# One store of 2 KB tiles for weights and work; output projections over 512 columns with their weights kept for both halves

## The chip, the cores and the metric

The kernel runs on one core of a Trainium2 chip. The metric is the device time of one execution in microseconds (us); the number given for a kernel is the median of its runs. Five engines share the work: TensorE (PE, matrix products, with its weight loads shown apart as PEld), VectorE (DVE), ScalarE (ACT), GpSimd (POOL) and SyncE (SP), which here issues nearly all transfers (DMA). Each engine runs its own instructions in a fixed order and waits on semaphores for the others.

## The reference

Four layers follow one another on one sequence of 1024 tokens of width 1024, all in float32: gated linear attention (gla), spatial gating (sgu), forgetting attention (fox), and gla again.

```python
cond = jax.nn.silu(c)
for i in range(DEPTH):                       # DEPTH = 4
    mod = (cond @ w_mod[i] + b_mod[i])[:, None, :]
    shift, scale, gate = jnp.split(mod, 3, axis=-1)
    h = rms_norm(x, norm_pre_g[i]) * (1.0 + scale) + shift
    kind, j = i % N_MIXERS, i // N_MIXERS
    if kind == 0:
        o = gla_mixer(h, gla_w_in[j], gla_w_a2[j], gla_b_a[j], gla_g_head[j], gla_w_out[j])
    elif kind == 1:
        o = sgu_mixer(h, sgu_w_in[j], sgu_ln_g[j], sgu_ln_b[j], sgu_w_s[j], sgu_b_s[j], sgu_w_out[j])
    else:
        o = fox_mixer(h, fox_w_in[j], fox_b_f[j], fox_g_q[j], fox_g_k[j], fox_w_out[j])
    x = x + gate * rms_norm(o, norm_post_g[i])
```

Each mixer begins with one wide product `h @ w_in` (3,088 columns for gla, 3,072 for sgu, 4,112 for fox) and ends with `(o * silu(z)) @ w_out` (1024 by 1024). These projections are most of the arithmetic. In sgu the `v` part of the product goes through a gelu and a layer norm over all of its 1024 columns.

## The kernel before

**Products.** A float32 product is made of three TensorE products: each operand is split into a high part in a shorter format and the low remainder, and `mm3` (L281) issues high by high (L283), high by low (L284 or L285) and low by high. For the activations the two parts are `hTh` and `hTl`, held for the whole layer, transposed, as 8 slices of 128 features. A token block is 128 tokens (8 of them, four to a half). `proj_tok` gives one token block times some columns of a weight, `proj_feat` gives 128 features times 512 tokens. Either runs over 8 slices `kt`, 24 matmuls in all, into one of three PSUM buffers called `pj`.

**Weights.** A weight is used in blocks of columns, usually 256. `load_w` (L244) brings a block in two pieces of 4 slices each (`wraw`, 128 partitions by 4 by 256, 512 KB, two buffers), ACT copies a piece to its high part `whi` (L252, CAST) and POOL subtracts for the low part `wlo` (L253). The parts lie in a pool of their own, `wp`, with 8 buffers under the tag `whl`. `getw` (L274) hands out the next block that the layer planned and starts the loads and splits of the one after it. The plan of a layer is made when that layer's code begins, so in program order nothing of the next layer's weights is asked for before the last projection of this one.

**Work tiles.** All other short-lived tiles come from a pool `sp` of 28 slots of 2 KB (per partition).

**Output projection.** `out_proj` (L397) goes through the two halves of the tokens; for each it fetches four blocks of 256 columns, so every block is loaded and split twice. For each block and each of 4 token blocks it makes a product of 256 columns, which DVE multiplies by the gate (L408) and ACT squares and sums (L410). When a half is done, `post` (L420) is queued as a filler, to be taken in steps between the products that follow: for each token block it loads `x` (L426), sums (L432), takes a reciprocal root on POOL (`rsq`, L337 and L338), adds to `x` in two pieces of 512 (L436), stores the new `x` (L440), and then starts the next layer's entry: a square and sum on ACT (L350), another `rsq`, a scaling on DVE, transposes on PE (L362) and the writing of `hTh` and `hTl`. So the second half's `post` runs beside the first projection of the next layer. The first projections of a layer need weights and the token blocks of the first half, which are ready by then.

**Order.** The program is built with a scheduler that simulates the engines and decides in which order each engine takes the instructions of the whole program, and when a pool's slot is handed to the next tile. The order on an engine can therefore differ from the order of the code, also across the end of a layer. A transfer waits on SP for the transfer issued eight before it, since there are eight semaphores for them.

## Time and profile before

| quantity | value |
|---|---|
| median of 3 runs | 2219.71 us (2216.93 to 2221.21) |
| profiled execution, device time | 2215.66 us |
| profiled execution, span of its trace | 2213.9 us |
| TensorE busy in the span | 2151.4 us, 97% |
| VectorE busy | 1367.9 us, 62% |
| ScalarE busy | 930.8 us, 42% |
| GpSimd busy | 903.1 us, 41% |
| mean granted TensorE clock | .993 of full speed |
| bytes moved by DMA | 217.54 MB, 98 GB/s |

The profile is of one execution. Busy times of the engines overlap, so they don't add up to the span; the chain of waits, followed back from the last instruction, tells which of them the end of the span rests on. A group in the view by line names line, engine, operation, what is written and read with its shape, the count, then total busy time and mean ns of one, then the idle time of the engine before these instructions and what ended it.

### The profile page before, as it was taken

What the parts mean: (1) busy time and instruction counts of PE and PEld (TensorE: products, weight loads), DVE (VectorE), ACT (ScalarE), POOL (GpSimd) and SP (SyncE); (2) the same over time, 40 slices, a digit from 0 to 9 for tenths busy, and PEclk for the clock granted to TensorE, in tenths of its full rate; (3) what the DMA queues carried; (4) which work ended last, traced back from release to release, by engine and by line L of the source; (5) the groups of instructions that cost most, each with busy time, mean ns of one, the idle gap of its engine ahead of it and who ended that gap; (6) DMA issues with size and microseconds to landing.
All of it is one profiled execution on the core that took longest, in us unless ns stands there. A gap on an engine that the chain in (4) does not pass through costs nothing.

```text
span 2213.9 us, 39277 instructions
## 1 busy us (share of the span) xinstructions
PE 2151.4 (97%) x15173; PEld 1938.8 (88%) x15173; DVE 1367.9 (62%) x3147; ACT 930.8 (42%) x1977; POOL 903.1 (41%) x767
## 2 busy tenths in 40 slices
PE   6999999999999999999999999999999999999998
PEld 6888889999998889998878888888689999899998
DVE  7586879635475425656555656656766675776633
ACT  4644333346321124554444434434556554333342
POOL 5433334366354324655144233232425451342363
PEclk9999999999999999999999999999999999999999
DMA  8122223335425324512222122112325320112334
GB/s 286 46 75 78 86 73 108 121 128 182 130 77 171 122 93 134 179 54 87 79 66 63 60 72 76 58 58 77 99 92 176 127 58 20 48 44 67 115 101 143
DMA packets 178150, 217.54 MB, mean 98 GB/s; under 512 B 13266, under 2 KB 128530, under 8 KB 177962
## 3 DMA queue, kind: packets, MB, share of 16 engines
q1 hardware_dynamic: 177962, 215.02, 30.9%
q8 instruction: 120, 1.97, 0.4%
q14 instruction: 68, 0.56, 0.1%
HBM read 185.03 MB, written 29.95 MB: 97 GB/s over the span
## 4 chain that ended last, share of the span: by engine, by line
PE 84%; DVE 12%; ACT 2%; issue 1%; DMA 1%; POOL 0%; DVEq 0%; POOLq 0%; SPq 0%; ACTq 0%
PE pj L283 21%; PE pj L284 21%; PE pj L285 21%; PE pm L1053 4%; PE pm L1042 3%; PE pb L1017 3%; PE pb L1016 2%; PE pb L621 2%; DVE md L195 2%; DVE s L578 1%; DVE s L610 1%; DVE s L600 1%; DVE s L606 1%; DVE s L603 1%; PE pm L362 1%
## 5 line engine op out<-in xcount | busy, mean ns | idle before, releaser
L283 PE MATMUL pj<-whi,hTh 128*128 128x256 f32 (+1 forms) x3072 | 893.0, 291 | 2.4 <-ACT junk L410 1.9
L285 PE MATMUL pj<-whi,hTl 128*128 128x256 f32 (+1 forms) x3072 | 883.0, 288 | 5.2 <-DVE hTl L385 3.0
L284 PE MATMUL pj<-wlo,hTh 128*128 128x256 f32 (+1 forms) x3072 | 880.9, 287 | 0.0
L253 POOL TENSOR_TENSOR wlo<-wraw,whi 128x1024 fp32r<-128x1024 f32 (+2 forms) x176 | 425.1, 2424 | 436.4 <-ACT whi L252 421.2
L283 PEld LDWEIGHTS pj<-whi,hTh 128*128 128x128 f32 x3072 | 589.0, 192 | 12.4 <-issue 5.1
L285 PEld LDWEIGHTS pj<-whi,hTl 128*128 128x128 f32 x3072 | 588.4, 192 | 12.9 <-issue 4.3
L284 PEld LDWEIGHTS pj<-wlo,hTh 128*128 128x128 f32 x3072 | 589.6, 192 | 6.7 <-issue 3.6
L283 PE MATMUL pj<-hTh,whi 128*128 128x512 f32 x640 | 255.5, 399 | 0.0
L284 PE MATMUL pj<-hTl,whi 128*128 128x512 f32 x640 | 254.4, 398 | 0.0
L285 PE MATMUL pj<-hTh,wlo 128*128 128x512 f32 x640 | 252.6, 395 | 0.0
L252 ACT CAST whi<-wraw 128x1024 fp32r<-128x1024 f32 (+2 forms) x176 | 177.8, 1011 | 133.8 <-PE pj L284 117.8
L195 DVE SCALAR_TENSOR_TENSOR md<-md,cond,md 128x512 f32<-128x512 f32 x184 | 175.3, 954 | 36.2 <-DMA md<-in_w_mod 34.5
L1010 POOL TENSOR_TENSOR db<-s,mneg 128x128 f32<-128x128 f32 x128 | 62.4, 499 | 243.1 <-DVE mx L1025 123.5
L1031 ACT ACTIVATE p<-p,ng 128x256 f32<-128x256 f32 (+7 forms) x128 | 99.6, 778 | 108.1 <-DVE ng L1029 107.2
L284 PEld LDWEIGHTS pj<-hTl,whi 128*128 128x128 f32 x640 | 120.8, 189 | 24.9 <-issue 2.3
L285 PEld LDWEIGHTS pj<-hTh,wlo 128*128 128x128 f32 x640 | 120.7, 189 | 24.8 <-issue 1.1
L283 PEld LDWEIGHTS pj<-hTh,whi 128*128 128x128 f32 x640 | 121.0, 189 | 24.3 <-issue 0.8
L1044 ACT COPY s<-pm 128x512 f32<-128x512 f32 (+2 forms) x192 | 87.1, 481 | 130.2 <-PE pm L1042 125.3
L408 DVE TENSOR_TENSOR s<-pj,gg 128x256 f32<-128x256 f32 x128 | 53.6, 421 | 136.2 <-PE pj L285 136.1
L1020 DVE CUSTOM_DVE_ANT_0 p<-pb,s 128x512 f32<-128x512 f32 (+3 forms) x160 | 83.5, 529 | 73.3 <-PE pb L1017 71.7
L338 POOL TENSOR_TENSOR r<-r,neghalf 128x1 f32<-128x1 f32 (+2 forms) x104 | 111.5, 1078 | 6.6
L410 ACT ACTIVATE junk<-pj 128x256 bf16<-128x256 f32 x128 | 49.2, 384 | 142.5 <-DVE s L408 139.4
(203 smaller groups left out, 3304.6 us busy)
## 6 DMA issues: line engine op xcount, KB each, us to landing
md<-in_w_mod SPq DMA_DIRECT2D x160, 256.0 KB
wraw<-in_gla_w_in SPq DMA_DIRECT2D x32, 512.0 KB
wraw<-in_gla_w_out SPq DMA_DIRECT2D x32, 512.0 KB
yd<-s SPq DMA_DIRECT2D x50, 256.0 KB
xd<-x SPq DMA_DIRECT2D x24, 512.0 KB
wraw<-in_sgu_w_in SPq DMA_DIRECT2D x24, 512.0 KB
x<-xd SPq DMA_DIRECT2D x24, 512.0 KB
wraw<-in_fox_w_in SPq DMA_DIRECT2D x48, 256.0 KB
```

Of the source, the lines that this page charges most:

```text
L195: ins = nc.vector.scalar_tensor_tensor(st["acc"], w[i], self.cond[:, kt:kt + 1], st["acc"], op0=ALU.mult, op1=ALU.add)
L252: nc.scalar.copy(hi, raw)
L253: nc.gpsimd.tensor_tensor(lo, raw, hi.bitcast(F32), op=ALU.subtract)
L283: nc.tensor.matmul(ps, lh, rh, start=first, stop=False)
L284: nc.tensor.matmul(ps, lh, rl, start=False, stop=False)
L285: nc.tensor.matmul(ps, ll, rh, start=False, stop=last)
L338: nc.gpsimd.tensor_tensor(r, r, self.half[:, 0:1].to_broadcast([P, n]) if n > 8 else self.half[:, 0:n], op=ALU.pow)
L1017: nc.tensor.matmul(sp[:, 0:w], q3[2][own[hb], qc], k2[own[hb], 0:w], start=False, stop=True)
L1020: nc.vector.tensor_tensor_reduce(e[:, c * 512:c * 512 + d0], sp[:, 0:d0], nf[p, c, hb][:, 0:d0], op0=ALU.add, op1=ALU.max, scale=1.0, scal ...
L1031: nc.scalar.activation(e[:, 0:n + P], e[:, 0:n + P], AF.Exp, bias=ng, accum_out=ls[:, 0:1])
L1044: nc.scalar.copy(et[:, 0:nb * P], pt[:, 0:nb * P])
L1053: nc.tensor.matmul(po[own[hb], 0:P], v[p, jb // 4][:, jb % 4, hb * 64:hb * 64 + 64], pts[hb][jb // 4][:, (jb % 4) * P:(jb % 4 + 1) * P], s ...
```

## The change

The pools `wp` are gone. One pool `sp` of 49 slots of 2 KB serves work tiles and weights. A block of a weight is loaded in tiles of 512 columns' worth: 4 tiles of two slices by 256 columns, or 8 tiles of one slice by 512, or by 272 where 16 more columns come along (then each tile takes two transfers). Each tile is cast on ACT (L262 after) and subtracted on POOL (L263 after) by itself.

The loads of the next block are no longer all emitted by `getw`; `prefetch` makes a list, and `wemit` takes some of it at slice 3 of each projection, in as many parts as `getw` was told calls. `getw` emits what is left.

`out_proj` works over 2 blocks of 512 columns per half in place of 4 of 256. In gla and sgu the first half's split weights stay in the store for the second half (`stay`), in fox they are loaded again. The `v` part of sgu is made in 512 columns instead of 256, first block for all 8 token blocks and then the second. The 512 KB loads of `w_mod` at the start become two of 256 KB.

Counts over the program: 3840 matmuls of 256 columns become 1920 of 512 (3072 of the 3840 in output projections, 768 in sgu's `v`). POOL's subtractions go from 154 of 1024 columns, 16 of 512 and 6 of 1088 to 276 of 512 and 24 of 272, and ACT's casts alike. The 128 evictions on L408 and the 128 on L410 become 64 each, of 512 columns. The transfers that SP issues rise from 667 to 857.

```diff
-        self.wp = pool("wp", 8)
-        self.sp = pool("sp", 28)
+        self.sp = pool("sp", 49)
...
-    def load_w(self, srcs, now=True):
+    def load_w(self, srcs):
         nc = self.nc
         ncol = sum(s.shape[1] for s in srcs)
-        raws, parts = [], []
...
+        g = max(1, 512 // ncol)
+        parts = {}
+
+        def load(i):
+            raw = self.s2([g, ncol])
             c = 0
             for s in srcs:
                 w = s.shape[1]
                 nc.sync.dma_start(out=raw[:, :, c:c + w],
-                                  in_=s[p4 * 512:(p4 + 1) * 512, :].rearrange("(k p) n -> p k n", p=P))
+                                  in_=s[i * g * P:(i + 1) * g * P, :].rearrange("(k p) n -> p k n", p=P))
                 c += w
...
+        def split(i, raw):
+            hi, lo = self.s2([g, ncol], F32R), self.s2([g, ncol], F32R)
+            nc.scalar.copy(hi, raw)
+            nc.gpsimd.tensor_tensor(lo, raw, hi.bitcast(F32), op=ALU.subtract)
+            parts[i] = (hi, lo)
...
-    def getw(self, ahead=1):
-        while len(self.wdone) < min(self.wnext + 1 + ahead, len(self.wseq)):
-            self.load_w(self.wseq[len(self.wdone)])
+    def prefetch(self, calls):
+        if len(self.wdone) == self.wnext and self.wnext < len(self.wseq):
+            load, split, n = self.load_w(self.wseq[self.wnext])
+            self.wq = [lambda i=i: split(i, load(i)) for i in range(n)]
+            self.wrate = -(-n // calls)
+
+    def wemit(self, n=None):
+        for _ in range(min(n or self.wrate, len(self.wq))):
+            self.wq.pop(0)()
+
+    def getw(self, calls=8, ahead=True):
+        if len(self.wdone) == self.wnext:
+            self.prefetch(1)
+        self.wemit(len(self.wq))
         w = self.wdone[self.wnext]
         self.wnext += 1
+        if ahead:
+            self.prefetch(calls)
         return w
...
     def out_proj(self, li, l, x_src):
...
-            for cb in range(4):
-                w = self.getw()
+            for cb in range(2):
+                if hf and self.stay:
+                    w = ws[cb]
+                    if cb:
+                        self.prefetch(4)
+                else:
+                    w = ws[cb] = self.getw(4, not (self.stay and cb))
                 for t in range(4):
-                    ps = self.proj_tok(w, hf * 4 + t, 256)
+                    ps = self.proj_tok(w, hf * 4 + t, 512, self.tick)
...
         def do_v(g, w, t):                          # sgu
-            ps = self.proj_tok(w, t, 256)
+            ps = self.proj_tok(w, t, 512, self.tick)
...
         for kind, i in order:                       # fox
-            w = self.getw()
+            w = self.getw(2 if kind == "z" else 8)
```

How the scheduler places the work changes at the end of each layer. The place shown is the hand-over from sgu to fox. First SP before: `wraw_9456` and `wraw_9463` are fox's first weights, `x_9527` and the like the token blocks of sgu's last half on their way in (L426) and out (L440).

```order
L426 DMA x_9527<-xd_130 128x1024
L261 DMA wraw_9220<-in_sgu_w_out 128x4x256
L426 DMA x_9529<-xd_130 128x1024
L261 DMA wraw_9456<-in_fox_w_in 128x4x256
L261 DMA wraw_9456<-in_fox_w_in 128x4x16
L261 DMA wraw_9463<-in_fox_w_in 128x4x256
L261 DMA wraw_9463<-in_fox_w_in 128x4x16
L261 DMA wraw_9470<-in_fox_w_in 128x4x128 x2
L261 DMA wraw_9477<-in_fox_w_in 128x4x128 x2
L440 DMA xd_131<-x_9527 128x1024
```

And SP after, where `s_1489_8531`, `s_1492_8538` and so on are fox's first weight tiles, and `x_8654`, `x_8671` and `x_8722` the second, third and fourth token block of sgu's last half (L449 in, L463 out):

```order
L463 DMA xd_128<-x_8654 128x1024
L449 DMA x_8722<-xd_127 128x1024
L463 DMA xd_128<-x_8671 128x1024
L255 DMA s_1489_8531<-in_fox_w_in 128x256
L255 DMA s_1489_8531<-in_fox_w_in 128x16
L255 DMA s_1492_8538<-in_fox_w_in 128x256
L255 DMA s_1492_8538<-in_fox_w_in 128x16
L255 DMA s_1495_8545<-in_fox_w_in 128x256
L255 DMA s_1495_8545<-in_fox_w_in 128x16
L463 DMA xd_128<-x_8722 128x1024
L255 DMA s_1498_8552<-in_fox_w_in 128x256
L255 DMA s_1498_8552<-in_fox_w_in 128x16
```

Fox's first weights stood ahead of every store of sgu's last token blocks; now the first three tiles stand behind the store of the third block and the rest behind that of the fourth. POOL before, at the same place (`wlo_9460` and `wlo_9467` are the low parts of fox's first weights, `r` the roots of `rsq` for sgu's last token blocks):

```order
L253 TENSOR_TENSOR wlo_9223<-wraw_9220,whi_9222 128x1024
L385 TENSOR_TENSOR hTl<-s_1346_9200,hTh 128x4x128
L253 TENSOR_TENSOR wlo_9460<-wraw_9456,whi_9459 128x1088
L253 TENSOR_TENSOR wlo_9467<-wraw_9463,whi_9466 128x1088
L337 TENSOR_SCALAR r_1390_9533<-ss_1389_9531 128x1
L338 TENSOR_TENSOR r_1390_9533<-r_1390_9533,neghalf 128x1
```

And POOL after (`r_1560` belongs to the entry of the third token block, `r_1572` and `r_1575` to the fourth's root and entry):

```order
L353 TENSOR_SCALAR r_1560_8815<-ss_1558_8812 128x1
L353 TENSOR_SCALAR r_1572_8915<-ss_1571_8913 128x1
L354 TENSOR_TENSOR r_1560_8815<-r_1560_8815,neghalf 128x1
L263 TENSOR_TENSOR s_1491_8535<-s_1489_8531,s_1490_8534 128x272
L354 TENSOR_TENSOR r_1572_8915<-r_1572_8915,neghalf 128x1
L263 TENSOR_TENSOR s_1494_8542<-s_1492_8538,s_1493_8541 128x272
L353 TENSOR_SCALAR r_1575_8924<-ss_1573_8921 128x1
L354 TENSOR_TENSOR r_1575_8924<-r_1575_8924,neghalf 128x1
L263 TENSOR_TENSOR s_1497_8549<-s_1495_8545,s_1496_8548 128x272
```

Both subtractions stood ahead of the roots of the last half; now three roots of the last two blocks stand between the first three. Last, PE before, from the last product of sgu (`pj_9415`) to the first of fox (`pj_9499`):

```order
L285 MATMUL pj_9415<-whi_9222,hTl 128x256
L283 MATMUL pj_9499<-whi_9459,hTh 128x272
L284 MATMUL pj_9499<-wlo_9460,hTh 128x272
L285 MATMUL pj_9499<-whi_9459,hTl 128x272
L283 MATMUL pj_9499<-whi_9459,hTh 128x272
```

And PE after (`pj_8490` is sgu's last product, `pm` the transposes of the first block of its last half, `pj_8618`, `pj_8673` and `pj_8724` fox's first three):

```order
L297 MATMUL pj_8490<-s_1420_7995,hTl 128x512
L378 MATMUL pm_8752<-ident,xn_8665 128x128 x4
L378 MATMUL pm_8757<-ident,xn_8665 128x128 x4
L295 MATMUL pj_8618<-s_1490_8534,hTh 128x272
L295 MATMUL pj_8673<-s_1490_8534,hTh 128x272
L295 MATMUL pj_8724<-s_1490_8534,hTh 128x272
L296 MATMUL pj_8618<-s_1491_8535,hTh 128x272
L297 MATMUL pj_8618<-s_1490_8534,hTl 128x272
L296 MATMUL pj_8673<-s_1491_8535,hTh 128x272
```

The first product of fox was made alone, slice after slice; now three token blocks are made side by side, nine matmuls for each weight tile. The hand-overs from gla to sgu and from fox to gla are arranged alike.

## Rows read from the trace of the kernel before

**Rows 1.** The page: busy time of each engine; shares of the chain of waits.
```profile
PE 2151.4 (97%) x15173; PEld 1938.8 (88%) x15173; DVE 1367.9 (62%) x3147; ACT 930.8 (42%) x1977; POOL 903.1 (41%) x767
...
PE 84%; DVE 12%; ACT 2%; issue 1%; DMA 1%; POOL 0%; DVEq 0%; POOLq 0%; SPq 0%; ACTq 0%
```

**Rows 2.** Windows: us, busy PE, PEld, DVE, ACT, POOL, granted clock, DMA, GB/s.
```profile
2150.00:2200.00 50.00, 50.00 (x419) 50.00 (x418) 15.25 (x30) 14.54 (x43) 22.02 (x18) 1.00 0.46 148
```

**Rows 3.** Timeline of PE (start, duration): ends of a 256-wide and a 512-wide run.
```profile
2131.56 0.36 PE L283 MATMUL pj<-whi,hTh 128*128 128x256 f32 x1
...
2206.39 0.28 PE L285 MATMUL pj<-whi,hTl 128*128 128x256 f32 x1
...
637.45 0.39 PE L283 MATMUL pj<-hTh,whi 128*128 128x512 f32 x1
...
658.99 0.39 PE L285 MATMUL pj<-hTh,wlo 128*128 128x512 f32 x1
```

**Rows 4.** Timelines of SP, ACT, POOL and PE at the hand-over from sgu to fox.
```profile
910.64 13.75 SPq L261 DMA_DIRECT2D wraw<-in_fox_w_in  x8
...
926.26 0.34 SPq L440 DMA_DIRECT2D xd<-x  x1
...
917.21 1.10 ACT L252 CAST whi<-wraw 128x1088 fp32r<-128x1088 f32 x1 [0.37 <-issue]
...
918.38 5.05 POOL L253 TENSOR_TENSOR wlo<-wraw,whi 128x1088 fp32r<-128x1088 f32 x2 [1.99 <-ACT whi L252]
...
929.92 0.28 PE L285 MATMUL pj<-whi,hTl 128*128 128x256 f32 x1
930.04 0.29 PE L283 MATMUL pj<-whi,hTh 128*128 128x272 f32 x1
```

**Rows 5.** By line and shape: count, busy us, mean ns, then idle before them.
```profile
L253 POOL TENSOR_TENSOR wlo<-wraw,whi 128x1024 fp32r<-128x1024 f32 x154 | 386.6, 2519 | 394.2 <-ACT whi L252 388.8 <-DMA yd<-s 2.0 <-PE pm L1042 2.0
L253 POOL TENSOR_TENSOR wlo<-wraw,whi 128x512 fp32r<-128x512 f32 x16 | 22.1, 1382 | 37.1 <-ACT whi L252 29.7 <-PE pj L285 6.9
L252 ACT CAST whi<-wraw 128x1024 fp32r<-128x1024 f32 x154 | 161.2, 1048 | 117.3 <-PE pj L284 103.8 <-issue 5.9 <-DMA wraw<-in_gla_w_in 3.9
L252 ACT CAST whi<-wraw 128x512 fp32r<-128x512 f32 x16 | 9.9, 620 | 14.1 <-PE pj L284 14.0
L350 ACT ACTIVATE xn<-x 128x1024 f32<-128x1024 f32 x24 | 25.4, 1060 | 32.7 <-DVE x L436 24.7 <-POOL wlo L253 2.7 <-issue 2.2
L338 POOL TENSOR_TENSOR r<-r,neghalf 128x1 f32<-128x1 f32 x72 | 47.4, 666 | 4.0
L408 DVE TENSOR_TENSOR s<-pj,gg 128x256 f32<-128x256 f32 x128 | 53.6, 421 | 136.2 <-PE pj L285 136.1
L1125 DVE SCALAR_TENSOR_TENSOR s<-s,pj 128x512 f32<-128x512 f32 x32 | 21.9, 684 | 38.3 <-ACT s L1124 38.1
```

**Rows 6.** Timeline of SP and DVE: a 256 KB load and what waits for it.
```profile
322.83 3.97 SPq L194 DMA_DIRECT2D md<-in_w_mod  x3
...
325.69 0.75 DVE L195 SCALAR_TENSOR_TENSOR md<-md,cond,md 128x512 f32<-128x512 f32 x1 [1.30 <-DMA md<-in_w_mod]
```

**Rows 7.** Chain of waits (start, duration): after the last matmul; at the start.
```profile
2206.56 0.13 PE pj L285
...
2208.61 0.19 POOL r L337
2209.47 0.75 DVE x L436
2210.22 0.66 DVEq L1220
...
10.74 4.58 DMA md<-in_w_mod
```

**Rows 8.** PE after an idle time: the window's granted clock, and its timeline.
```profile
836.20:839.60 3.40, 3.39 (x16) 3.39 (x17) 2.46 (x4) 0.62 (x1) 0.00 (x0) 0.50 0.94 311
...
835.01 0.50 PE L285 MATMUL pj<-whi,hTl 128*128 128x256 f32 x2 [1.69 <-DVE hTl L472]
```

103 lines of the change are left out of this document (48 added, 55 removed).

## The prediction

> **What bounds the kernel now.** I read the page's first part and its chain first: TensorE (PE) is busy 2151.4 of 2213.9 us, and the chain of waits runs over it for 84% [rows 1]. No other engine is busy for more than 62%, so a change pays through what PE's own instructions take and through its gaps. The view by windows of an output projection says it plainer: PE is busy 50.00 of 50 us at clock 1.00 while DVE has 15, ACT 14.5 and POOL 22 us of work [rows 2]. The question for each edit is therefore whether PE gets shorter, or is made to wait where it now doesn't. The places where it could are the ends of the layers. There the timelines show fox's first weights issued on SP at 910.64, cast at 917.21 and subtracted from 918.38 on, while sgu's last stores come later, from 926.26; PE goes from sgu's last product, 929.92, to fox's first, 930.04, without a gap [rows 4].
>
> **The change, part by part.**
>
> *A. Wider products.* PE's timeline has a run of 624 matmuls of 256 columns from 2131.56 to 2206.39: 74.83 / 623 = 120.1 ns from start to start. A run of 96 of 512 columns goes from 637.45 to 658.99: 21.54 / 95 = 226.7 ns [rows 3]. One of 512 in place of two of 256 saves 2 x 120.1 - 226.7 = 13.5 ns, and 1920 pairs are joined: **-25.9 us**, all on PE and so on the path. It is the surest term; if every tenth new product waited for something else it would be -23.
>
> The Trainium skill, page TensorE: Matmul & The Clock Gate, section Back-to-back issue gap, gives the gap of a single matmul at full clock as N / 2.4 + 2.5 ns, 109 ns for 256 columns and 216 for 512. The two runs above disagree by 11 ns in each. By the page A would be an estimated 1920 x 2.5 = 5 us and the whole forecast 21 us more.
>
> *B. The hand-overs.* In the new order the next layer's first weights stand behind the last token blocks' `post`: the loads behind their stores on SP, the subtractions behind their roots on POOL, the casts behind their squares on ACT. The square writes a buffer that is freed by transposes on PE after the last product. I work it out from the rows, with 0 at the end of these transposes. A cast takes 0.62 us for 512 columns and 1.05 for 1024, so 0.42 for 272; a subtraction 1.38 and 2.52, so 0.85 for 272; a square 1.06, a root's second step 0.67 [rows 5] and its first 0.19; an addition to `x` 0.75 [rows 7]. A transfer of 256 KB lands 2.86 us after its issue (322.83 to 325.69) [rows 6]. From a block's last matmul to the end of its additions pass 3.66 us (2206.56 to 2210.22) [rows 7].
> Sgu to fox: the square ends at 1.06, two first steps and one second step at 2.1, the first subtraction at 3.0. PE wants it after three matmuls, at 0.4. The fourth block's root ends at 3.7, the second subtraction at 4.5, the two additions at 5.2, its square at 6.3, its root at 7.2, and behind that on POOL the third subtraction at 8.0. Without waits PE would be there after 21 matmuls, at 2.7: 5.3 us. The fourth tile is issued behind the store at 5.2, lands at 8.1, is cast at 8.5 and subtracted at 9.4, about where PE comes to it; with half a dozen hand-overs between engines, 6.2.
> Gla to sgu: tiles of 512, so 2.04 us of PE for each, which hides more. First subtraction at 1.06 + 0.38 + 1.33 + 1.38 = 4.2 against 1.1 wanted, 3.1; the third tile's load stands behind the fourth block's store (4.3), so lands at 7.2 and is ready at 9.2 against 8.4, and an `x` load stands before the next ones: 5.
> Fox to gla: on SP a load of `x` waits for the transposes, and behind it the first weight tile: issued at 0.7, landed at 3.6, or 4.0 since 512 KB go ahead, cast at 4.4, subtracted at 5.3 against 0.4; the third tile's load stands behind the store of the last block, whose `x` came at 4.0: additions 5.5, landing 8.8, ready at 10.0 against 7.6. With the hand-overs, 8.
> Together **+19.2**. If only the first wait of each place is real, 2.6 + 3.1 + 4.9 = 10.6; if the loads land another 2.9 us late at all three, 28. I take the middle, since the second waits follow from the order on one engine.
>
> *C. The clock after a gap.* Behind an idle time of 1.69 us PE worked 3.40 us at a granted clock of 0.50, the 1.2 GHz level [rows 8]. This costs 1.7 us. The three hand-overs each have one longer gap or more: 5.1, of which some falls into time that PE waits for tiles anyway. I take **+3.5**, 0 to 9.
>
> *D. Three products side by side* end together, so three evictions of 0.42 to 0.68 us [rows 5] come at once and the fourth product waits for one of only three buffers: 3 x 0.7, **+2** (0.5 to 3).
>
> *E. Fox's blocks behind a z block.* A z block has two projections in which to ask for the next weights, and in the new order the last tile's split follows 13 to 20 matmuls ahead of its use, 2.9 us at 226.7 ns. Cast and subtraction take 0.62 + 1.38 = 2.0 [rows 5]. With one more subtraction ahead on POOL it is 3.4: 0.43 late. Ten such blocks: **+4.3**; 0 if nothing is ahead, 9 if half of them have two ahead.
>
> *F. Start.* Twelve more transfers stand ahead of the first `w_mod` load, which is now issued at 10.74 and heads the chain of the start [rows 7]. At 0.34 us an issue (926.26) [rows 4] that is 4.1 late at most; the bytes are the same, so **+2**, 0 to 4.1.
>
> *G. Tail.* The last eviction is 512 wide: 0.68 for 0.42 on DVE [rows 5], the square alike: **+0.5**.
>
> *Without cost:* the smaller splits (two of 512 take 0.25 us more on POOL and 0.19 more on ACT than one of 1024 [rows 5]) where POOL and ACT are less than half busy [rows 2]; the halved loads of output weights bring nothing, since no product of a projection waited for them.
>
> Sum: -25.9 + 19.2 + 3.5 + 2 + 4.3 + 2 + 0.5 = +5.6. The profiled execution took 2215.66, so 2221.3; the median of the runs is 4.05 above that execution: **2225**.
>
> **The rivals.**
> *R1, faster.* The hand-overs wait, but not long: squares and roots of the last blocks are done when PE arrives, because PE itself arrives later or because the order on POOL was drawn too dark here. 8 us for the three, 1 each for C, D, E and F: -25.9 + 12 = -13.9, **2206**. For it speaks that A is measured and the costs are inferred; against it the transposes, after which the square can't be earlier. It decides when B to G stay under 21 us.
> *R2, no change.* First waits only (10.6), C to G as taken (12.3): -3.0, **2217**; up to the sum of all with B at 16 it stays within 0.2%, which is 4.4 us and about what a measurement of this kernel can tell from no change.
> *R3, slower by a percent.* PE goes through the eight tiles of each hand-over at the 1.2 GHz level, since tile by tile it waits again: 72 matmuls of 0.13 to 0.23 us cost their own length once more, 9.4 + 16.3 + 9.4 = 35 at most, 24 with what is hidden by the waits, in place of 3.5: **2246**. It decides where the granted clock stays 0.50 over the whole stretch and not for 3.4 us. Against it: in rows 8 the clock came back.
> *R4, the wide matmul brings nothing.* The 512-wide run of rows 3 is of `proj_feat`, whose weights are the loaded operand; the 256-wide one is of `proj_tok`, whose activations are. No row shows a `proj_tok` of 512. If one took twice 120.1, A would be 0 and the time **2251**; half of A, 2238. Against it: both forms load 128 by 128 and stream the rest. The page's 5 us lies near this end, and the trace doesn't bear out its figures.
> That the change doesn't do what it says can be left out, as the counts of the program are known.
>
> **How the numbers follow.** My forecast's mechanism, with its sizes about as taken, has 0.48; R1 0.27, R2 0.15, R3 0.07, R4 0.03. Slower by over 0.2% means above 2224.1: most of the forecast's own spread, a third of which lies just under that line, with R3 and R4: 0.45. Faster means under 2215.3: R1 and a little of R2, 0.30. The rest, 0.25, is within 0.2%. The forecast's own range, from its bounds with not all at one end, is 2216 to 2240. To hold the time 8 times in 10 the range reaches down to R1 and up to R3's edge: 2206 to 2244.
>
> **What the changed profile would show.** A: in output projections 227 ns from start to start, L432 and L433 with 64 instructions each. B: at three places PE idle, ended by the casts on L262 or the subtractions on L263, and three token blocks side by side; 5, 6 and 8 us. C: granted clock under 1 in the windows behind them only. D: a fourth product released by an eviction. E: in fox, PE idle ended by L262 or L263 at the first product of a block. F: the first projection later than in the trace of before by 2 us. The prediction is wrong if the idle time at the hand-overs is under 10 us in all, or if PE waits most in places named nowhere here, such as the middle of a layer, for a slot of the shared store.

## The result, and the profile of the changed kernel

The changed kernel takes **2288.85 us** (median of 4 runs, 2280.52 to 2296.14), the kernel before, run beside it, 2218.32 (4 runs, 2214.39 to 2221.21). The ratio is 1.0318, with a 95% interval from 1.0279 to 1.0357: slower by 3.2%, some 70 us. The forecast was 2225 with a range of 2206 to 2244, and the time lies above that range.

The page's first part and the clock of the profiled execution (device time 2287.94 us) answer to [rows 1]. Columns: busy us, share of the span, instructions.

```profile
PE 2162.4 (95%) x13253; PEld 1854.7 (81%) x13253; DVE 1308.6 (57%) x3083; ACT 903.4 (40%) x1957; POOL 863.6 (38%) x891
```
```profile
core 0: 2286.2 us, clock 0.976
```

PE's busy time rose by 11.0 us, though 1920 matmuls fewer are issued: the mean granted clock is .976 of full speed where it was .993.

The view of an output projection answers to [rows 2]: us, busy time of PE, PEld, DVE, ACT and POOL, granted clock, DMA share, GB/s. Under it, PE's timeline in the last output projection (start, duration) answers to [rows 3].

```profile
2200.00:2250.00 50.00, 50.00 (x230) 41.58 (x229) 14.70 (x25) 11.33 (x28) 18.86 (x20) 1.00 0.29 94
```
```profile
2224.66 0.39 PE L295 MATMUL pj<-s,hTh 128*128 128x512 f32 x1
2224.88 0.39 PE L296 MATMUL pj<-s,hTh 128*128 128x512 f32 x1
```

PE is busy throughout at full clock, with 230 matmuls where there were 419. A wide product follows the one before it by 0.22 to 0.23 us; over 293 of them in this stage the mean is 66.28 / 292 = 227.0 ns.

So the wide products do what they should, and the time goes elsewhere. The next table cuts both traces at the same points of the program: the first projection, and the last eviction of each layer's output projection (L408 before, L432 after). "Idle" is the sum of PE's gaps in a stage, from its first instruction on. "Clock" is half of PE's busy time in stretches at a granted clock of 0.50, which is what these stretches cost against full speed.

| stage | before, us (idle, clock) | after, us (idle, clock) | difference |
|---|---|---|---|
| start, to the first projection | 48.2 (15.2, 0) | 65.7 (32.3, 0) | **+17.5** |
| gla | 495.4 (19.0, 6.5) | 489.3 (17.6, 8.1) | -6.1 |
| sgu | 389.3 (2.0, 1.7) | 384.6 (7.0, 1.5) | -4.7 |
| fox | 805.2 (7.1, 1.7) | 858.4 (35.9, 25.2) | **+53.2** |
| last gla | 468.6 (9.1, 4.0) | 481.3 (21.3, 7.9) | **+12.7** |
| tail | 7.2 | 7.0 | -0.3 |
| span | 2213.9 (52.4, 14.0) | 2286.2 (114.0, 42.7) | +72.3 |

61.6 us more of idle time and 28.7 more lost to the clock, less 25.3 for the products (below), make 65.0 of the 72.3; 7 us, most of them in fox, stay unexplained. Where PE waits is listed by what ended the wait (total us, times, longest). First the kernel before, then after:

```profile
PE pj L285 <- DVE hTl L385: 3.0, 2, 1.5
...
PE pb L190 <- DMA md<-in_w_mod: 2.7, 3, 2.3
```

```profile
PE pj L295 <- ACT s L262: 17.2, 7, 6.2
PE pb L190 <- DMA s<-in_w_mod: 10.9, 1, 10.9
...
PE pb L205 <- DVE md L195: 8.1, 2, 7.8
PE pm L1071 <- ACT s L1062: 7.7, 2, 7.5
...
PE pj L295 <- ACT hTh L494: 3.8, 2, 3.3
```

L295 to L297 are the products of a projection. Before, no wait of a projection was longer than 1.7 us. After, they wait for casts of weights (L262), for the activations' high parts (`hTh`) and for evictions (`junk`, L433: 3.7 us), and attention for its own copies (L1062); all of these run on ACT. The next view shows why ACT is late. It sums the idle time of ACT right ahead of the weights' casts by what ended it (us, times), for L252 before and for L262 after.

```profile
  PE pj L284: 117.8, 92
```

```profile
  DMA s<-in_sgu_w_in: 73.1, 28
  DMA s<-in_gla_w_in: 48.2, 31
  DMA s<-in_fox_w_in: 39.2, 27
  DMA s<-in_fox_w_out: 26.3, 10
  DMA s<-in_gla_w_out: 11.8, 6
```

Before, a cast stood on ACT waiting for the buffer that it writes to be freed by PE (117.8 us, 92 times), and for its own load 5.2 us in three cases. After, ACT stands 198.6 us in 102 cases waiting for the cast's own load to land, 1.9 us each. ACT takes its instructions in order, so whatever is behind such a cast is held up as well.

### The profile page after: what moved, and what is told of

Same layout as the page of the kernel before. It is cut to its first block, busy times and chain, and to the rows that moved or that the text cites. A ratio compares the mean times of both kernels' runs of the same rounds, so it can differ in the third digit from the quotient of the medians.

```text
span 2286.2 us, 35893 instructions
## 1 busy us (share of the span) xinstructions
PE 2162.4 (95%) x13253; PEld 1854.7 (81%) x13253; DVE 1308.6 (57%) x3083; ACT 903.4 (40%) x1957; POOL 863.6 (38%) x891
## 5 line engine op out<-in xcount | busy, mean ns | idle before, releaser
L295 PE MATMUL pj<-s,hTh 128*128 128x256 f32 (+2 forms) x2432 | 777.6, 325 | 35.5 <-ACT s L262 17.2
L296 PE MATMUL pj<-s,hTh 128*128 128x256 f32 (+2 forms) x2432 | 777.0, 320 | 3.2 <-POOL s L263 3.0
L297 PE MATMUL pj<-s,hTl 128*128 128x256 f32 (+2 forms) x2432 | 773.3, 320 | 3.0 <-DVE hTl L495 3.0
L263 POOL TENSOR_TENSOR s<-s,s 128x512 fp32r<-128x512 f32 (+1 forms) x300 | 397.9, 1335 | 573.6 <-ACT s L262 535.2
L295 PEld LDWEIGHTS pj<-s,hTh 128*128 128x128 f32 x2432 | 467.0, 194 | 77.0 <-ACT s L262 19.8
L296 PEld LDWEIGHTS pj<-s,hTh 128*128 128x128 f32 x2432 | 471.1, 194 | 35.7 <-POOL s L263 5.4
L297 PEld LDWEIGHTS pj<-s,hTl 128*128 128x128 f32 x2432 | 470.7, 194 | 33.7 <-DVE hTl L495 3.7
L295 PE MATMUL pj<-hTh,s 128*128 128x512 f32 x640 | 255.9, 400 | 0.0
L262 ACT CAST s<-s 128x512 fp32r<-128x512 f32 (+1 forms) x300 | 176.9, 600 | 199.1 <-DMA s<-in_sgu_w_in 73.1
L296 PE MATMUL pj<-hTl,s 128*128 128x512 f32 x640 | 253.5, 396 | 0.0
L297 PE MATMUL pj<-hTh,s 128*128 128x512 f32 x640 | 253.4, 396 | 0.0
L297 PEld LDWEIGHTS pj<-hTh,s 128*128 128x128 f32 x640 | 121.0, 189 | 25.4 <-issue 0.8
L1062 ACT COPY s<-pm 128x512 f32<-128x512 f32 (+2 forms) x192 | 86.6, 480 | 137.4 <-PE pm L1060 136.9
L295 PEld LDWEIGHTS pj<-hTh,s 128*128 128x128 f32 x640 | 121.2, 189 | 24.3 <-issue 0.8
L296 PEld LDWEIGHTS pj<-hTl,s 128*128 128x128 f32 x640 | 121.0, 189 | 24.4 <-issue 1.6
```

What stands on the lines that cost most here:

```text
L262: nc.scalar.copy(hi, raw)
L263: nc.gpsimd.tensor_tensor(lo, raw, hi.bitcast(F32), op=ALU.subtract)
L295: nc.tensor.matmul(ps, lh, rh, start=first, stop=False)
L296: nc.tensor.matmul(ps, lh, rl, start=False, stop=False)
L297: nc.tensor.matmul(ps, ll, rh, start=False, stop=last)
L1062: nc.scalar.copy(et[:, 0:nb * P], pt[:, 0:nb * P])
```

## The experiments

The theories, in the order in which they came: that the order at the hand-overs and late asking make PE wait; as rivals, that wide products bring nothing, and that the store is too full; and when these had fallen or explained a part only, that raw tiles sharing the store tie each cast to its own load. Stages are cut as in the table above. Where an expectation speaks of time lost to the clock, it counts half of the whole stretch at 0.50, idle time in it included (56 us for the changed kernel); the text counts PE's busy time there (42.7). Where a kernel ran once, its time stands beside one run of the kernel before on the same chip; those runs lay between 2208.83 and 2222.26 us, and 13 runs of it on one chip between 2208.96 and 2230.71 (median 2217.62), so differences of less than some 20 us are read from the traces and not from the times.

### Are the wide products a gain?

*e1_narrow*: the changed kernel, with output projections in products of 256 columns again; the weights are loaded, split and kept as changed, only asked for over twice as many products of the output projections.

```diff
-                    ps = self.proj_tok(w, hf * 4 + t, 512, self.tick)
+                for i in range(2):
+                    wi = lambda kt, w=w, i=i: tuple(x[:, i * 256:(i + 1) * 256] for x in w(kt))
...
+                        ps = self.proj_tok(wi, hf * 4 + t, 256)
```

> The changed kernel with its output projections made 256 columns at a time again (each kept or loaded tile of 512 columns is used in two products; sgu's v stays at 512). In the order that results the next layers' first weights stand ahead of the last products again, 60 matmuls or more. Theory (the late weights at the three hand-overs cost 23 us of idle time and some 15 us of half clock behind it; the wide products save 13.5 ns for each of 1536 pairs, 21 us): 2288.9 + 21 - 38 = 2272. Rival 1 (the wide products save nothing here): 2251. Rival 2 (the hand-overs are not what costs, the tile-wise splitting is): 2310.

2301.33 us (before 2219.19). The four output projections take 94.4, 90.9, 132.8 and 88.5 us from first to last eviction, 32.4 more than in the changed kernel together. The whole span is 13.4 longer: idle 3.1 more, but 13.2 less lost to the clock, so that the products by themselves are 23 us longer, where 1536 pairs at 2 x 120.1 - 227.0 = 13.2 ns give 20. The theory that wide products bring nothing falls.

*e8_store*: the store of 49 slots and the tile-wise loads alone; all blocks are 256 wide as before, and each output weight is loaded for both halves.

```diff
+        n = 2 if stay else 4
...
-            for cb in range(2):
-                self.plan([w_out[:, cb * 512:(cb + 1) * 512]])
+            for cb in range(n):
+                self.plan([w_out[:, cb * (D // n):(cb + 1) * (D // n)]])
...
-        self.plan_out(w_out)
+        self.plan_out(w_out, False)
...
-            ps = self.proj_tok(w, t, 512, self.tick)
+            ps = self.proj_tok(w, t, 256)
```

> One part of the change alone: the one store of 49 slots, weights loaded and split tile by tile, but all products and blocks 256 columns wide as before and output weights loaded for each half. Theory (the store and the small tiles by themselves cost the start, 17 us, and little else): 2219 + 20 = 2240. Rival (small tiles on ACT, POOL and SP are what costs): 2288.9 + 26 = 2315, with idle time spread over all layers.

2335.8 us (before 2220.11): 116 us slower than before. The store with its way of asking for weights costs more than the whole change, and wide products with kept weights give 47 us of it back.

### The order at the hand-overs

*e2_early*: the next layer's first block is planned beside the last products of the output projection, so that its loads and splits are no longer behind `post`.

```diff
...
             for cb in range(2):
+                if hf and cb and nxt is not None:
+                    self.plan_first(nxt)
```

> The changed kernel, and the first weight block of the next layer is planned and asked for already beside the last products of a layer. Theory (late weights at the hand-overs): the idle time at the three places, 6.6 + 7.5 + 9.0 us, and the half clock behind it, some 15 us, go: 2288.9 - 38 = 2251. Rival (the early loads only push other loads and splits back, in a store without free slots): over 2280. Against the kernel with narrow products, which has early weights too, this one shows what the wide products are worth: 21 us faster if they save 13.5 ns a pair, the same if nothing.

2281.95 us (before 2219.19). Gla and sgu together are 9.0 us shorter, and sgu has no idle time left: there the order was the cause. At fox's hand-over another wait took its place. PE's timeline at the first products of fox, and DVE's:

```profile
949.21 0.56 PE L311 MATMUL pj<-s,hTh 128*128 128x272 f32 x1 [8.51 <-DVE al L965]
```
```profile
943.16 0.75 DVE L384 TENSOR_SCALAR xn<-x,r 128x1024 f32<-128x1024 f32 x1 [9.62 <-POOL r L370]
```

PE has filled its three buffers and stands 8.51 us until `al` (L965) is copied out of the first. DVE is behind in order: it waited 9.62 us for a root. The square that this root needs writes a buffer that transposes must free, and PE comes to these only behind its first products of fox (PE, then ACT):

```profile
939.67 1.04 PE L394 MATMUL pm<-ident,xn 128*128 128x128 f32 x8
```
```profile
940.80 1.06 ACT L382 ACTIVATE xn<-x 128x1024 f32<-128x1024 f32 x1 [2.33 <-PE pm L394]
```

Five casts of the new weights ahead of the square had waited 1.40 + 3.37 + 1.91 + 0.81 + 0.54 = 8.0 us for their loads, but they were done at 938.47, so it is the order on PE that made this wait. At the last gla there is a like wait of 8.60 us, and 49.6 us are lost to the clock in all. Asking early moves the wait on, to another place in the order.

### The start

*e3_start*: only half of the first block's 16 transfers are issued ahead of `w_mod`.

```diff
-        raws = [load(i) for i in range(nw)]
+        raws = []
...
+                for i in range(nw // 2 * (n // 2), nw // 2 * (n // 2 + 1)):
+                    raws.append(load(i))
```

> The changed kernel, only the start: the second half of the first weight block is loaded just ahead of its split and not ahead of all else, so 8 instead of 16 small transfers stand before the first w_mod load. Theory (the start's 17.5 us come from the many transfers issued ahead of w_mod on SP): the first projection comes 8 us earlier or more, 2280 or less. Rival (the start is held by the bytes or by DVE's w_mod sums, not by the order on SP): first projection within 2 us of the changed kernel's 65.67, 2289.

2276.24 us (before 2219.19); the start takes 58.0 us, 7.6 less. Fox is 7.1 us shorter as well, with 7.1 us less lost to the clock, though no line of fox was touched: the clock can differ where the code doesn't.

*b1_mod256*: the kernel before, with `w_mod` in loads of 256 KB into the same tiles.

```diff
-                    self.last["sp"] = nc.sync.dma_start(out=wt, in_=a["w_mod"][l, 2 * kp * P:(2 * kp + 2) * P, j * 512:(j + 1) * 512]
-                                      .rearrange("(i p) n -> p i n", p=P))
+                    for i in range(2):
+                        self.last["sp"] = nc.sync.dma_start(out=wt[:, i, :], in_=a["w_mod"][l, (2 * kp + i) * P:(2 * kp + i + 1) * P,
+                                                                                            j * 512:(j + 1) * 512])
```

> The kernel before, with each 512 KB load of w_mod at the start issued as two of 256 KB into the same buffer. Theory (a transfer waits for the one eight before it, so halving them halves the bytes in flight, and the start is bound by that): the first projection 7 us later or more, 2226. Rival (the start's loss is the 16 weight transfers ahead of w_mod alone): first projection within 2 us of 48.19, 2219.

2220.56 us (before 2220.11); the start takes 48.3 us. The smaller transfers of `w_mod` cost nothing.

*b4_start16*: pool and tiles as in b2_tiles below, the first block in 16 transfers.

```diff
+                if now:
+                    nc.sync.dma_start(out=raw[:, :, c:c + w],
+                                      in_=s[p2 * 256:(p2 + 1) * 256, :].rearrange("(k p) n -> p k n", p=P))
+                else:
+                    for k in range(2):
+                        nc.sync.dma_start(out=raw[:, k, c:c + w], in_=s[(2 * p2 + k) * P:(2 * p2 + k + 1) * P, :])
```

> The kernel before with its own weight pool in half-size buffers, but the first weight block brought in 16 transfers of one slice each (128 KB and 8 KB) into the same 4 raw buffers, in place of 8. Theory (the number of small transfers ahead of w_mod sets the start): first projection at 55 or later, 2219. Rival (only the order against w_mod counts): within 2 us of 48.6, 2212.

2216.79 us (before 2222.26). The start takes 51.2 us against 48.6 of b2_tiles, so 2.6 us come from the number of transfers. The rest of the 17.5 has other causes, one of which SP's and POOL's timelines of the changed kernel show; the last fence is SP in b4_start16.

```profile
37.91 11.92 SPq L181 DMA_DIRECT2D s<-in_w_mod  x8
```
```profile
42.63 8.48 POOL L263 TENSOR_TENSOR s<-s,s 128x272 fp32r<-128x272 f32 x8 [3.83 <-ACT s L262]
```

```profile
34.75 6.07 SPq L181 DMA_DIRECT2D md<-in_w_mod  x8
```

The last eight loads of `w_mod` take 11.92 us to issue, where they take 6.07 with a pool of their own. In the changed kernel they need slots of the store; SP's waits there are ended four times by POOL's subtractions of the first block (7.4 us), whose run of 8.48 us begins only at 42.63. PE then waits 7.8 us for the modulation made of these loads (the longest of the 8.1 in the rows of PE's waits above), where the kernel before waited 1.4. PE's wait of 10.9 us for `w_mod` is another one: it ends at 20.99, before any subtraction. There the first product with `w_mod` stands on PE ahead of the transposes of `x`, which begin at 23.47 where they began at 10.63, and with them the squares, casts and subtractions come later. How the 15 us divide between this order and the slots was not measured.

### What the waits in the middle depend on

*e4_whole*: all loads and splits of the next block are asked for at the first projection.

```diff
-            self.wrate = -(-n // calls)
+            self.wrate = n
```

> The changed kernel, but all tiles of the next weight block are asked for at once, at the first product of the block before it, as in the kernel before, instead of spread over its products. Theory (in fox the late splits bunch the attention pieces, which leaves TensorE idle and at half clock for 30 us): fox is 15 us or more shorter, 2272. Rival (the bunching comes from the shared store's slots, or from the start of fox): fox within 5 us of the changed kernel's, 2284 to 2292.

2333.87 us (before 2219.19), 45 us worse than the changed kernel, with 151 us idle. Asking for loads and splits together and earlier makes it worse in this store.

*e6_sp45*: 45 slots in place of 49.

```diff
-        self.sp = pool("sp", 49)
+        self.sp = pool("sp", 45)
```

> The changed kernel with 45 slots in the store in place of 49; every engine's instructions stand in the same order as in the changed kernel, only what frees a slot, and so the waits, differ. Theory (the store is full where the time is lost: around the output projections, where two blocks of 512 columns want 32 slots): 2305 or more, with the growth at the end of fox's attention and in its output projection. Rival (the order of the instructions makes the waits, slots are not short): within 5 us of 2288.9.

2286.16 us (before 2220.11): the same as with 49, and every engine has its instructions in the same order. My theory that the store is too full falls: four slots fewer cost nothing.

*e7_fox256*: fox's output projection in blocks of 256 as before.

```diff
+        n = 2 if stay else 4
         for _ in range(1 if stay else 2):
-            for cb in range(2):
-                self.plan([w_out[:, cb * 512:(cb + 1) * 512]])
+            for cb in range(n):
+                self.plan([w_out[:, cb * (D // n):(cb + 1) * (D // n)]])
...
```

> The changed kernel, but fox's output projection in blocks of 256 columns as before (4 tiles of weights, 8 slots a block, loaded again for the second half), the other layers unchanged. Theory (fox's wide blocks don't fit beside attention's tiles): the stall at the end of attention (13 us idle, 7 at half clock) and the 24 us that fox's output projection lost go, the hand-over to the last layer (9 us) too, and 384 pairs x 13.5 ns = 5 us come back: 2288.9 - 45 = 2244. Rival (those stalls come from the order on ACT and SP whatever the width): 2285 to 2295.

2284.99 us (before 2220.11). This was to take away the wait at the end of fox's attention, which in the changed kernel looks like this (ACT, then SP, then PE):

```profile
1624.87 0.62 ACT L262 CAST s<-s 128x512 fp32r<-128x512 f32 x1 [3.21 <-DMA s<-in_fox_w_out]
1625.39 0.85 ACT L1062 COPY s<-pm 128x512 f32<-128x512 f32 x2
```
```profile
1621.35 0.33 SPq L194 DMA_DIRECT2D md<-in_w_mod  x1
1621.72 0.42 SPq L255 DMA_DIRECT2D s<-in_fox_w_out  x1
```
```profile
1626.02 1.33 PE L1071 MATMUL pm<-s,s 128*64 128x128 f32 x10 [7.47 <-ACT s L1062]
```

The load of an output weight is issued at 1621.72, behind a load of the next layer's `w_mod`. Its cast waits 3.21 us on ACT until it lands, and the copy behind the cast (L1062), which has nothing to do with weights, is what PE then waits 7.47 us for; about 4 of these are the cast's, since ACT was free for the copy at 1621. With blocks of 256 this wait is gone and fox is 9.2 us shorter, but the last gla is 3.7 and the first 2.0 longer, and the span is 3.8 shorter in all. One wait of many was removed.

*e9_ahead*: the loads of a block are asked for at its start, the splits in parts as changed.

```diff
-            self.wq = [lambda i=i: split(i, load(i)) for i in range(n)]
+            raws = [load(i) for i in range(n)]
+            self.wq = [lambda i=i: split(i, raws[i]) for i in range(n)]
```

> The changed kernel, but all loads of the next weight block are asked for when its turn to be fetched begins, and only the splits are spread over the products of the block before. In the changed kernel ACT sat idle for 199 us ahead of weight casts until their load landed (5 us in the kernel before), with evictions and attention's copies queued behind. Theory (these waits of the casts make TensorE's waits and the bunches of attention pieces): that idle time falls under 60 us, and the time to 2255. Rival (the casts wait where ACT has nothing else to do; the order on the engines costs): 2280 to 2295.

2271.08 us (before 2208.83): some 18 us better than the changed kernel, or 8 if each is taken against the kernel before beside it. In the traces the span is 16.9 us shorter, 11.9 of it idle time. ACT's idle time ended by a cast's own load falls from 198.6 us to 55 (51.8 of it in the row below). It removes most of that wait and at most a quarter of the loss, so most of ACT's waiting cost PE nothing.

*e10_all*: the three edits of e9_ahead, e2_early and e3_start together.

> Three edits together on the changed kernel: loads ahead of their splits, the first block of the next layer asked for beside a layer's last products, half of the start's weights loaded behind w_mod. Theory (the losses add up): 2288.9 - 34 - 7 - 13 = 2235. Rival (each only moves the waits to the next place): over 2260.

2239.77 us (before 2208.83), with 88.6 us idle and 19.8 lost to the clock. Mending the order at three places gets back 49 of the 70 us, or 40 against the kernel before beside it, and doesn't reach that kernel. By the traces 25 us of the gain are idle time and 23 are clock.

### Tile size, asking, or the store?

*b2_tiles*: the kernel before, its pool `wp` kept, with tiles of half the size: 16 buffers for parts, 4 for raw tiles, and `w_mod` at the start in loads of 256 KB.

```diff
-        self.wp = pool("wp", 8)
+        self.wp = pool("wp", 16)
...
-        for p4 in range(2):
-            raw = self.wp.tile([P, 4, ncol], F32, tag="wraw", name=self.nm("wraw"), bufs=2)
+        for p2 in range(4):
+            raw = self.wp.tile([P, 2, ncol], F32, tag="wraw", name=self.nm("wraw"), bufs=4)
```

> The kernel before with its own weight pool, but weights loaded and split in four pieces of 2 slices a block in place of two of 4 (16 buffers of half the size, raw pieces 4 in place of 2; w_mod in 256 KB loads). Asked for at the same place of the program as before. Theory (the size of the tiles is not what costs; the late asking and the shared store are): 2219 to 2226. Rival (small pieces cost by themselves: more transfers and more waits on ACT and POOL): 2240 or more.

2211.83 us (before 2208.83).

*b3_spread* goes further: pool and tiles of b2_tiles, with the changed kernel's `prefetch` and `wemit`, so weights are asked for as late as there.

```diff
-        while len(self.wdone) < min(self.wnext + 1 + ahead, len(self.wseq)):
-            self.load_w(self.wseq[len(self.wdone)])
+        if len(self.wdone) == self.wnext:
+            self.prefetch(1)
+        self.wemit(len(self.wq))
...
+            if kt == 3:
+                self.wemit()
```

> The kernel before with its own weight pool in half-size buffers (2211.8), but asking for the next block as the changed kernel does: one piece at slice 3 of each product of the block before, with the same numbers of calls. Theory (the one store is what costs, not the asking): 2209 to 2222. Rival (asking late costs): 2240 or more.

2211.62 us (before 2222.26). Neither the small tiles nor the late asking costs anything while raw tiles and split tiles have buffers of their own. e8_store, with the same widths, tile sizes and asking, differs from this kernel in little but the one store, and is 124 us slower: the store is what costs.

*e12_once* takes the store of e8_store and asks for each next block as the kernel before does, whole and at once.

```diff
         if ahead:
-            self.prefetch(calls)
+            self.prefetch(1)
+            self.wemit(len(self.wq))
```

> The store alone with 256-wide blocks (2335.8), but each block is loaded and split at once when the block before it begins, as in the kernel before, in place of spread over that block's products. Theory (asking late is the cause): 2245, the start's 17 us and little else. Rival (that all tiles share one store is the cause: the order in which slots are taken): 2310 or more.

2405.33 us (before 2208.83): the worst of all, by 193 us against b2_tiles, from which it differs in little but the store. PE is idle for 203 us.

*e13_onceraw* is e12_once with four buffers for raw tiles of their own, and 44 slots for the rest; *f1_raw* is e9_ahead with the same four buffers.

```diff
-        self.sp = pool("sp", 49)
+        self.wp = pool("wp", 4)
+        self.sp = pool("sp", 44)
...
-            raw = self.s2([g, ncol])
+            raw = self.wp.tile([P, g, ncol], F32, tag="wraw", name=self.nm("wraw"))
```

> The slowest of these kernels (one store, 256-wide blocks, each block asked for at once: 2405.3) with its raw tiles in 4 buffers of their own, the store at 44 slots. Theory (raw and split tiles from one store tie each cast to its own load, and so hold up ACT): ACT's idle time ahead of weight casts ended by a DMA falls from 256 us to under 60, the time to 2290 or less. Rival (split tiles take the work tiles' slots): over 2350.

> The changed kernel with the raw weight tiles in 4 buffers of their own (the store has 44 slots) and all loads of a block asked for when its turn to be fetched begins: a load then waits for a raw buffer alone, and may run ahead of its cast as in the kernel before. Theory (sharing slots between raw and split tiles ties each cast to the landing of its own load): ACT's idle time ahead of weight casts ended by a DMA under 20 us (199 in the changed kernel), and 2250 or less. Rival (that split tiles share slots with work tiles is what costs): that idle time falls, but the time stays over 2265.

2282.51 us (before 2222.26) and 2263.13 (before 2217.62). The view by line and shape shows the casts of 512 columns: count, busy us, mean ns, then ACT's idle time before them and what ended most of it. f1_raw falls short of its expectation: it is 26 us below the changed kernel and still 45 above the kernel before, 22 of these at its start (70.0 us against 48.2). The rows, in order: changed kernel, e9_ahead, f1_raw; then e12_once, e13_onceraw, b2_tiles.

```profile
L262 ACT CAST s<-s 128x512 fp32r<-128x512 f32 x276 | 167.6, 616 | 185.7 <-DMA s<-in_sgu_w_in 73.1 <-DMA s<-in_gla_w_in 39.2 <-DMA s<-in_fox_w_in 34.9
```
```profile
L262 ACT CAST s<-s 128x512 fp32r<-128x512 f32 x276 | 165.7, 617 | 51.8 <-DMA s<-in_sgu_w_in 30.7 <-DMA s<-in_fox_w_in 10.0 <-DMA s<-in_gla_w_in 5.6
```
```profile
L263 ACT CAST s<-wraw 128x512 fp32r<-128x512 f32 x276 | 166.0, 617 | 21.3 <-DMA wraw<-in_gla_w_in 7.5 <-DMA wraw<-in_fox_w_in 5.2 <-DMA wraw<-in_sgu_w_in 4.8
```
```profile
L262 ACT CAST s<-s 128x512 fp32r<-128x512 f32 x324 | 193.1, 615 | 255.8 <-DMA s<-in_sgu_w_in 82.1 <-DMA s<-in_fox_w_in 45.1 <-DMA s<-in_gla_w_in 42.7
```
```profile
L263 ACT CAST s<-wraw 128x512 fp32r<-128x512 f32 x324 | 187.9, 617 | 41.0 <-DMA wraw<-in_gla_w_in 12.6 <-DMA wraw<-in_sgu_w_in 10.0 <-DMA wraw<-in_gla_w_out 6.7
```
```profile
L252 ACT CAST whi<-wraw 128x512 fp32r<-128x512 f32 x308 | 187.1, 619 | 83.6 <-PE pj L284 71.8 <-POOL wlo L253 2.6 <-DMA wraw<-in_gla_w_in 1.6
```

A cast takes 615 to 619 ns in all of them; what differs is the wait ahead of it. With raw tiles in the store it is ended by the load (185.7 us here, 255.8 in e12_once). With raw tiles in buffers of their own 41.0 us remain of the 255.8, and the kernel is 123 us faster, with one slot fewer in all and nothing else changed in the code. In b2_tiles the wait is ended by PE (`pj`), as in the kernel before, and by loads for 2 us; b3_spread's row reads the same (83.2 us, 73.4 of them by PE).

What held the loads themselves stands in SP's waits (total us, times, longest). First a line of the kernel before, then two of the changed kernel, where L194 is a load of `w_mod`:

```profile
SPq L261 <- POOL wlo L253: 797.9, 117, 38.1
```
```profile
SPq L194 <- DVE md L195: 306.9, 96, 25.7
...
SPq L255 <- PE pj L296: 64.5, 10, 15.6
```

With buffers of their own, SP stands at the next weight load until POOL's subtraction frees a raw buffer: 797.9 us in the kernel before, 874.0 in b2_tiles, 931.2 in e13_onceraw. The raw tiles of the next block land while the present one is used, well ahead of their casts. In the changed kernel POOL's subtractions end only 51.9 us of such waits. Of the 102 loads that held up a cast, 20 had last been held on SP by a wait of a weight load (24.2 of the 198.6 us); 81 stood right behind another transfer that had to wait, 31 of them behind a load of `w_mod` (92.9 us) and 19 behind a store of `x` (26.2 us). Such a load is issued late, and its cast waits for it.

So the loads come late mostly by their place in SP's order, which the scheduler makes from the pools that it is given, and less because a slot for them is missing when the program runs. This fits e6_sp45, with the same order and the same time. That sharing buffers between raw tiles and the rest brings these waits is shown by e12_once against e13_onceraw and b2_tiles. Why the scheduler places the loads so late then was not followed.

e13_onceraw is still 70 us behind b2_tiles; 24 us of it are its start (72.7 against 48.6 us). The rest stays open. Split tiles and work tiles share slots there, which was not undone by itself; but f5_wide below keeps 16 split tiles in the store of work tiles without such a loss.

### A version that takes the gain alone

*f5_wide*: b2_tiles, with the output projections of both gla layers and of sgu in 512 columns. One half of their split weights is kept in the pool of weights, the other in 16 slots of the store; fox's output projection and sgu's `v` stay at 256.

```diff
+        if wide:
+            for cb in range(2):
+                self.plan([w_out[:, cb * 512:(cb + 1) * 512]], cb == 1)
+            return
...
+            if store:
+                return self.s2([g, ncol], F32R)
+            return self.wp.tile([P, g, ncol], F32R, tag="whl", name=self.nm(name))
```

> The kernel before with its own weight pool in half-size buffers, and output projections over 512 columns in gla, sgu and gla, their split weights kept for both halves: the first 512 columns lie in the weight pool's 16 buffers, the second in 16 slots of the 28-slot store. Fox and sgu's v stay 256 wide; the squares stay 256 wide. Theory (the wide products pay 13.5 ns a pair, and the one store is what ate it): 1152 pairs, 15.6 us, 2203, ratio 0.993. Rival (kept weights starve the work tiles of slots in any pool, so `post` and the next layer wait): 2219 or more.

**2203.95 us** (median of 10 runs, 2195.75 to 2210.7) against 2217.62 of the kernel before (13 runs, 2208.96 to 2230.71): a ratio of 0.9936, 95% from 0.9915 to 0.9958. It beats both kernels, the one before by 0.6%.

Against b2_tiles the three layers with wide products are 2.4, 6.2 and 3.5 us shorter, 12.1 in all, where 1152 pairs at 13.2 ns give 15.2. Fox, whose code is the same, is 5.1 us longer, with 6.9 more lost to the clock, so the whole gains less than the three layers.

## Why the prediction was wrong, step by step

Three steps failed: "Without cost", which gave the splits from a shared pool no term, the start (F) and the clock (C).

**A, the wider products: right.** 227.0 ns measured, 226.7 taken: 1920 x 13.2 = 25.3 us for 25.9. The row of `proj_feat` stood for the new `proj_tok`, and R4 is refuted. The page TensorE: Matmul & The Clock Gate of the Trainium skill, section Back-to-back issue gap, gives an estimated 215.8 ns for one isolated matmul of 512 columns; the trace disagrees by 11 ns, as in [rows 3].

**B, the hand-overs: right.** Gla to sgu, sgu to fox, fox to gla, from PE's timeline:

```profile
558.96 0.96 PE L295 MATMUL pj<-s,hTh 128*128 128x512 f32 x3 [2.72 <-ACT s L262]
560.63 0.50 PE L296 MATMUL pj<-s,hTh 128*128 128x512 f32 x1 [0.70 <-POOL s L263]
...
567.46 0.96 PE L295 MATMUL pj<-s,hTh 128*128 128x512 f32 x3 [3.14 <-ACT s L262]
568.82 0.80 PE L296 MATMUL pj<-s,hTh 128*128 128x512 f32 x1 [0.40 <-POOL s L263]
```
```profile
943.00 0.64 PE L295 MATMUL pj<-s,hTh 128*128 128x272 f32 x3 [2.57 <-ACT s L262]
944.05 0.60 PE L296 MATMUL pj<-s,hTh 128*128 128x272 f32 x1 [0.41 <-POOL s L263]
...
948.57 0.65 PE L295 MATMUL pj<-s,hTh 128*128 128x272 f32 x3 [0.94 <-ACT s L262]
949.89 0.39 PE L296 MATMUL pj<-s,hTh 128*128 128x272 f32 x1 [0.68 <-POOL s L263]
...
961.55 0.56 PE L295 MATMUL pj<-s,hTh 128*128 128x272 f32 x1 [3.27 <-DVE al L947]
```
```profile
1805.05 1.05 PE L295 MATMUL pj<-s,hTh 128*128 128x272 f32 x3 [6.23 <-ACT s L262]
...
1811.35 1.05 PE L295 MATMUL pj<-s,hTh 128*128 128x272 f32 x3 [1.42 <-ACT s L262]
...
1822.65 0.39 PE L295 MATMUL pj<-s,hTh 128*128 128x272 f32 x1 [1.37 <-DVE al L557]
```

Waits for casts and subtractions: 2.72 + 0.70 + 3.14 + 0.40 = 7.0 us (5 forecast), 2.57 + 0.41 + 0.94 + 0.68 = 4.6 (6.2), 6.23 + 1.42 = 7.7 (8). Together 19.2, as forecast; the single places are off by 2 us at most, and that the sum agrees to the tenth is chance. Working out each place from the order of SP, ACT and POOL, with durations of [rows 5 to 7], held. R1 and R2, in which less of it was real, are refuted.

**D, bunched evictions**: 3.27 + 1.37 = 4.6 us (waits for `al`), forecast 2, at most 3.

**E, late splits in fox: wrong.** PE waits for casts 17.2 us in 7 cases, and 17.0 of these are the six at the hand-overs above; in the blocks of fox's mixer it waits for none, so the term is about 0 and not 4.3. The step took an order on POOL for a wait.

**F, start: wrong**, 17.5 us for 2. I priced the twelve transfers at their issue, which b4_start16 shows to be right (2.6 us). What I left out is that `w_mod` now takes its slots from the store (those loads go to `s2` tiles), so that its last loads wait for the subtractions of the first block, and that the order on PE at the start changes with it, transposes of `x` from 23.47 on where they stood at 10.63. The shares of the two stay open.

**"Without cost: the smaller splits": wrong, a cost that was put at nothing.** I compared the duration of casts and subtractions with the slack of ACT and POOL, and the slack was there: the casts take as long as forecast, and ACT is busy 40% of the span. The cost isn't their duration but that each stands on an in-order engine until its load lands, 198.6 us for 5.2. PE's idle time in fox outside the hand-over, which had no term, is 28.0 us, where all of fox had 7.1: some 21 more. I had asked who waits for the cast, and not who stands behind it: evictions, the attention's copies and `hTh`. In fox's output projection that reads, ACT first, then PE:

```profile
1731.84 0.62 ACT L262 CAST s<-s 128x512 fp32r<-128x512 f32 x1 [2.46 <-DMA s<-in_fox_w_out]
...
1740.97 0.62 ACT L262 CAST s<-s 128x512 fp32r<-128x512 f32 x1 [2.59 <-DMA s<-in_fox_w_out]
```
```profile
1733.60 0.80 PE L295 MATMUL pj<-s,hTh 128*128 128x512 f32 x1 [3.27 <-ACT hTh L494]
...
1737.80 0.80 PE L297 MATMUL pj<-s,hTl 128*128 128x512 f32 x1 [2.97 <-DVE hTl L495]
...
1742.22 0.79 PE L295 MATMUL pj<-s,hTh 128*128 128x512 f32 x1 [2.35 <-ACT junk L433]
```

Two casts wait 2.46 and 2.59 us for `fox_w_out`, and PE waits 3.27, 2.97 and 2.35 for the parts of activations (ACT, and DVE behind it) and for the eviction by ACT, not for the weights. The prediction's last sentence named such places ("the middle of a layer, for a slot of the shared store") as what would make it wrong, without a price or a chance.

**C, the clock: wrong by a factor of eight**, 28.7 us more lost (42.7 for 14.0) where 3.5 were taken and 9 was the bound. C and R3 had priced half clock at the hand-overs only. Behind these it took 1.5, 6.4 and 5.6 us, 13.5 together, which alone is more than the bound. Windows (columns as above) at a fall in fox's attention and behind the hand-over from fox to gla, with PE's timeline at the first (the ends of matmuls are modelled in these records, so that PE may be less busy than they say):

```profile
1070.00:1080.00 10.00, 9.21 (x56) 6.07 (x55) 8.22 (x28) 2.81 (x6) 1.89 (x3) 1.00 0.16 53
1080.00:1090.00 10.00, 10.00 (x26) 5.54 (x26) 5.86 (x25) 4.40 (x8) 1.46 (x1) 0.52 0.25 80
1804.00:1817.00 13.00, 10.47 (x42) 9.72 (x43) 2.51 (x3) 3.74 (x9) 7.68 (x11) 0.50 0.65 183
```
```profile
1079.96 1.20 PE L1060 MATMUL pm<-ident,p 128*128 128x128 f32 x6 [0.74 <-DVE p L1051]
```

Behind the hand-over the clock is 0.50 for the whole of 13 us, which is R3's mechanism at one of its three places. But the larger part is in fox (25.2 us for 1.7, with 6.4 of it behind the hand-over from sgu). There a gap of 0.74 us is followed by 13.7 us at 0.50, and PE has no gap in the window shown (busy 10.00 of 10.00). What PE does there are the attention's products (`pb`, `pm`); of projections (`pj`) there is 0.80 us in that window. In the kernel before, attention pieces stood between long projections, and fox lost 1.7 us. It is shown that the time was lost there, and that it comes and goes between kernels (fox loses 6.6 us in e10_all and 34.3 in e2_early). That the bunching of attention without projections between is the cause is only argued; what made the clock fall stays open.

**G**: the tail is 0.3 us shorter where 0.5 longer was forecast. The range failed because every bound was drawn round a place that I had found in the order; the cost of sharing buffers, present at every block, had no term. In sum, C came out 25 us above the forecast, F 15, and the waits in fox's middle 21 above nothing; these three make the miss, with A and B where they were forecast. How much of the 21 the casts' waits make is not shown; e9_ahead, which takes 144 of the 198.6 us away, is 17 us shorter in all.

## What to carry to other kernels

Before buffers of two kinds are put into one pool, ask for each transfer which instruction frees its slot and what stands behind the first instruction that reads it: landing buffers that shared a pool with work tiles turned prefetching into waiting here, since their loads came to stand late in the queue of transfers, and on an in-order engine part of that wait is paid by work that never needed the data. Price an added instruction by the wait it may hold its engine for, not by its duration against that engine's slack. And a gain that is measured per instruction, as 13 ns a pair here, is worth taking by the smallest edit that carries it.
